# Moving the GpSimd additions of the first three pairs of an MLP product to VectorE

## Chip, cores and metric

The kernel runs on one core of a Trainium2 chip. The metric is device time in microseconds for one launch: the median of the runs shown. Beside it stands one profiled execution, from which the rows of the profile come. The engines are TensorE (PE in the profile; its weight loads PEld), VectorE (DVE), ScalarE (ACT), GpSimd (POOL) and SyncE (SP), whose queue issues the loads and stores.

## What is computed

Two layers of a hybrid block on 1024 latent tokens and 256 context tokens of width 1024. Each layer has a modulated norm, an input projection, a mixture of attention, Fourier and gated position mixing, an output projection with a gated residual, and then the part that matters here:

```python
def squared_relu_mlp(h, w1, w2):
    return jnp.square(jax.nn.relu(h @ w1)) @ w2

x = x + gt1 * mix_x
x = x + gt2 * squared_relu_mlp(modulate(rms_norm(x, g2), sh2, sc2), w1, w2)
```

`w1` is 1024 x 4096. The context goes through the same weights in layer 0 only; layer 1 (`last` in the code) leaves it out. Everything is float32.

## The kernel before

**Precision.** A float32 product is made of three TensorE products: each operand is split into a rounded part `h` (a ScalarE copy that rounds) and a rest `lo` (a VectorE subtraction), and `h*h`, `h*lo`, `lo*h` are summed in PSUM. So every operand tile costs one ScalarE and one VectorE instruction of 128x512 before TensorE can use it.

**Quads and blocks.** The latent tokens form two quads of 512 tokens (`QUADS`). The first MLP product is done by Strassen's scheme on 2 x 2 blocks: the features in two halves of four 128-chunks, the tokens in two quads, and the 4096 columns of `w1` in pairs (block `p` and block `p + NP`, `NP` = 16), so that 7 block products replace 8. Its operand sums are formed once for the tokens (lists `ysum[1..7]`) and once per pair for the weights (`split_block`). The stages that the change touches, in the order of the code:

- `mix_out` (L1329) adds the output projection to the residual and calls `square_sum` (L502, L503): ScalarE squares a chunk, GpSimd adds it to the quad's sum of squares. The sum over all 8 chunks (`KC`) goes through ones-matmuls (L522) to the row statistics.
- `norm_first` and `norm_second` modulate the chunks of quad 0 and quad 1 (`modulated`, L1470 and L1471), form the sums of chunks (`y_sum`, L1482) and split each into `h` (L1476) and `lo` (L1477) in `y_split`. `c in YSUM`, which is chunk 1 or 3, goes to GpSimd, the others to VectorE; all four sums of `norm_first` carry the number 1.
- `split_block` forms a weight sum (L1582; on GpSimd for the products named in `FSUM` from pair 2 on) and splits it (L1584, L1586).
- `first_product` issues the 12 matmuls of one block product (L1672 to L1674; context L1658 to L1660).
- `after_product` copies products 2, 5, 1 from PSUM (L1688), forms their sums (L1690 on VectorE, L1692 on GpSimd, L1696, L1700, L1703, L1707 from PSUM on VectorE) and applies the squared ReLU (L1643, L1644).
- `combine` forms five sums (L1635) of a pair's four result blocks, the operand sums of the second product, and stores them; sums number 1 and 3 (`POOLT`) are on GpSimd.

The order of products is a list written out by hand, `seq`: products of the first three pairs (0, 1, 2) are interleaved, since the token sums are still being formed; `norm_second` is a generator (`side2`) stepped beside the first two pairs by `ahead_of`, and weight splits run three items ahead. From pair 3 on all operands of the tokens exist. The order in each engine's queue is not the order of the source: a scheduler orders the instructions before they are run, by readiness and by their place in the source. Each queue is then run in order.

Of the kernel before, what the change touches and what calls it, by code (L numbers as in the profile page):

```python
# [15 lines left out]
ALU = mybir.AluOpType  # L16
# [4 lines left out]
KC = D // P  # L21
# [6 lines left out]
NP = NFF // 2  # L28
POOLT = (1, 3)
FSUM = ((2, 1, 6), (2, 6))  # L30
YSUM = (1, 3)
HD = 64
NH = 8
EPS = 1e-6
# [95 lines left out]
def hybrid_block_kernel(ctx: ExitStack, tc: tile.TileContext, a: dict, out: bass.AP):  # L130
# [10 lines left out]
    def alloc(tag, shape, dt):  # L141
        cnt[0] += 1
        tag_of[f"{tag}_{cnt[0]}"] = tag
        return sb.tile([P] + list(shape), dt, tag=tag, bufs=BUFS[tag], name=f"{tag}_{cnt[0]}")
# [7 lines left out]
    def T(*shape, dt=F32R):  # L152
        return alloc("T", shape, dt)

    def M(*shape, dt=F32):
        return alloc("M", shape, dt)
# [9 lines left out]
    def PB(*shape, dt=F32):  # L166
        cnt[0] += 1
        tag_of[f"pB_{cnt[0]}"] = "B"
        return ps.tile([P] + list(shape), dt, tag="B", bufs=8, name=f"pB_{cnt[0]}")
# [4 lines left out]
    V, A, E, G = nc.vector, nc.scalar, nc.tensor, nc.gpsimd  # L174
# [20 lines left out]
    def mm3(o, lh, ll, rh, rl, first, last):  # L195
        E.matmul(o, lh, rh, start=first, stop=False)  # L196
        E.matmul(o, lh, rl, start=False, stop=False)  # L197
        E.matmul(o, ll, rh, start=False, stop=last)  # L198
# [293 lines left out]
            y[1].append(lo)  # L492
            yield

    def square_sum(acc, x, k):

        w = x.w
        if k == 0:
            A.activation(acc[:, :w], x.chunk(k), AF.Square)
        else:  # L500
            sq = M(512)
            A.activation(sq[:, :w], x.chunk(k), AF.Square)  # L502
            G.tensor_tensor(acc[:, :w], acc[:, :w], sq[:, :w], ALU.add)  # L503

    def norm(x, acc, mod, j, y, pool=False):

# [116 lines left out]
    def layer(l, ys, norms, bank):  # L623
# [84 lines left out]
        for pi in range(5):  # L708
            ts = (2 * pi, 2 * pi + 1)
            w = 512 if ts[0] in tiles else 256  # L710
# [607 lines left out]
        def mix_out(x, wts, qi, d):  # L1318

            hs, ls = wts  # L1320
            o = PB(512)
            for i, k in enumerate(MIX_ORDER):
                f = slice((k % 4) * P, (k % 4 + 1) * P)
                mm3(o[:, :x.w], hs[k // 4][:, f], ls[k // 4][:, f], *mix[qi, k], i == 0, i == KC - 1)
                if i % 3 == 2:
                    yield
            yield
            j = 0 if qi < 2 else 1
            V.scalar_tensor_tensor(x.chunk(d), o[:, :x.w], mods[l, 2][:, j, d:d + 1], x.chunk(d), ALU.mult, ALU.add)  # L1329
            square_sum(ssum[qi], x, d)  # L1330

        class Two(Rows):

# [4 lines left out]
        ssum = {}  # L1338

        def early_out(qs):  # L1340

            x = {}
            for qi in qs:
                yield from split_mix(qi, MIX_ORDER)
                ssum[qi] = S(512)
                x[qi] = Two(qi)
                xmid[qi] = DR(f"xm_{l}_{qi}", P, KC * x[qi].w)
            ahead = [split_rows(a["w_out"][l], 0, WTAG[0], G if WG[l] else V)]
            for d in range(KC):
                wts = ahead.pop(0)  # L1350
                if d + 1 < KC:
                    ahead.append(split_rows(a["w_out"][l], d + 1, WTAG[(d + 1) % 2], G if WG[l] else V))
                for qi in qs:
                    if d % 2 == 0:
                        w = x[qi].w
                        t = R(2, w) if qi == 0 else S(2, w)
                        load(flat(t), xdram[l, qi][:, d * w:(d + 2) * w])
                        x[qi].t.append(t)
                yield
                for qi in qs:  # L1360
                    yield from mix_out(x[qi], wts, qi, d)
                    if d % 2:
                        w = x[qi].w
                        store(xmid[qi][:, (d - 1) * w:(d + 1) * w], flat(x[qi].t[d // 2]))
            yield from split_mix(1, [k for k in MIX_ORDER if k != 3])
            wout.append(split_rows(a["w_out"][l], 0, WTAG[0]))
            yield
            wout.append(split_rows(a["w_out"][l], 1, WTAG[1]))
            yield
# [110 lines left out]
        def y_sum(c, x, y, op):  # L1480
            t = M(512)
            (G if c in YSUM else V).tensor_tensor(t, x, y, op)  # L1482
            return t
# [110 lines left out]
        for d in range(KC):  # L1594
            if d + 2 < KC:
                wout.append(split_rows(a["w_out"][l], d + 2, WTAG[d % 2]))
            if d == KC - 3:
                w1_load(0, 0)
                w1_load(1, 0)
                w1_load(0, 1)  # L1600
                w1_load(2, 1, "T")
                split_block(5, 0, "T")
            if d == KC - 2:
                w1_load(1, 1)
                split_block(5, 1, "T")
                split_next()
                split_next()
            if d == KC - 1:
                split_next()
            for i, _ in enumerate(mix_out(xm[1], wout[d], 1, d)):  # L1610
                step(side)
                if last and i == 1 and d:
                    to_tokens(1, d - 1)
            if d % 2 and not last:
                store(xmid[1][:, (d - 1) * 512:(d + 1) * 512], flat(xm[1].t[d // 2]))
# [7 lines left out]
        def put(i, p, t):  # L1623
            store(tdram[i][:, p * 512:(p + 1) * 512], t)

        def combine(p):

            b11, b12, b21, b22 = (hq.pop((p, b)) for b in (11, 12, 21, 22))
            put(2, p, b11)
            put(5, p, b22)  # L1630
            for n, (i, x, y, op) in enumerate(((4, b21, b11, ALU.subtract), (3, b12, b22, ALU.subtract),
                                               (1, b11, b22, ALU.add), (6, b11, b12, ALU.add),
                                               (7, b21, b22, ALU.add))):
                t = alloc("W2", [512], F32)
                (G if n in POOLT else V).tensor_tensor(t, x, y, op)  # L1635
                put(i, p, t)

        fbank, fsum = {}, {}
        BANK = {2: "a", 4: "a", 5: "g", 3: "g", 1: "b", 7: "b", 6: "d"}

        def relu2(p, b, src, t=None):
            t = t or T(512, dt=F32)
            A.activation(t, src, AF.Relu)  # L1643
            A.activation(t, t, AF.Square)  # L1644
            hq[p, b] = t
# [38 lines left out]
        def after_product(i, p):  # L1684
            o = fbank[p, BANK[i]]
            if i in (2, 5, 1):
                m = fsum[p, i] = alloc("T" if (i, p) == (2, 2) else "W2", [512], F32)
                A.copy(m, o)  # L1688
            if i == 5:
                V.tensor_tensor(fsum[p, 2], fsum[p, 2], fsum[p, 5], ALU.add)  # L1690
            if i == 1:
                G.tensor_tensor(fsum[p, 1], fsum[p, 1], fsum[p, 2], ALU.subtract)  # L1692
            if i in (4, 5):
                fsum[p, "n"] = fsum.get((p, "n"), 0) + 1
                if fsum[p, "n"] == 2:
                    V.tensor_tensor(fsum[p, 5], fbank[p, "a"], fsum[p, 2], ALU.subtract)  # L1696
                    relu2(p, 21, fbank[p, "a"])
            if i == 7:
                t = T(512, dt=F32)
                V.tensor_add(t, o, fsum[p, 5])  # L1700
                relu2(p, 11, t, t)
            if i == 3:
                V.tensor_add(fsum[p, 1], o, fsum[p, 1])  # L1703
                relu2(p, 12, o)
            if i == 6:
                t = T(512, dt=F32)
                V.tensor_add(t, o, fsum[p, 1])  # L1707
                relu2(p, 22, t, t)
                combine(p)
# [166 lines left out]
        def finish_quad(qi):  # L1876

            x = xm[qi]
            nsum[qi] = S(512)
            for k in range(KC):  # L1880
                square_sum(nsum[qi], x, k)
                yield
            keep(l + 1, qi, x)
            nnorm[qi] = norm(x, nsum[qi], lambda: (mods[l + 1, 1], mods[l + 1, 0]), 0 if qi < 2 else 1, ny[qi],
                             qi == 0)
            if qi == 0:
                yield from nnorm[0]
# [45 lines left out]
        if not last:  # L1933
            finish_bg()

            x = xm[2]
# [94 lines left out]
```

## Time and profile before

| quantity | value |
|---|---|
| runs | 2709.23, 2714.17, 2719.12 us; median 2714.17 |
| profiled execution | 2711.95 us, span 2710.2 us |
| mean granted TensorE clock | 0.989 |
| GpSimd instructions | 773 |
| VectorE instructions | 3709 |
| L1482 on GpSimd | 24 of 40, median 1.30 us, longest 5.29 us |
| L1482 on VectorE | 16 of 40, median 0.68 us, longest 1.78 us |

Times in the profile are microseconds unless marked ns; `pB` is a PSUM tile, all other names are tiles in SBUF or tensors in DRAM. "idle before" is the engine's idle time ahead of a group and, behind the arrow, the instruction that ended it. A chain is the sequence of work that ended last, each piece released by the one before it.

### The profile page before, as it was taken

The numbers are of one execution on the slowest core, as the hardware profiler recorded it, in microseconds if no ns is written. First come the engines' busy times: TensorE is split into PE (matmuls) and PEld (weight loads), VectorE is DVE, ScalarE is ACT, GpSimd is POOL, SyncE is SP. The second block draws the span as 40 slices with busy tenths as digits, with TensorE's granted clock in tenths as the row PEclk, the third lists the DMA queues.
The fourth block names the chain that finished last, engine by engine and source line by source line (L and its number), as shares of the span: only waits on it lengthen the run. The fifth ranks groups of instructions, "written<-read, shape, count | busy, mean of one in ns | idle before, by whom it ended". The sixth has DMA issues, their size and how long they took to land.

```text
span 2710.2 us, 39517 instructions
## 1 busy us (share of the span) xinstructions
PE 2597.2 (96%) x13236; PEld 2140.0 (79%) x13236; DVE 2177.7 (80%) x3709; ACT 1526.1 (56%) x3248; POOL 1013.1 (37%) x773
## 2 busy tenths in 40 slices
PE   7998899999989999999999999899999899999999
PEld 4777687787768888888879987787886688888877
DVE  7897979768998998689887674888676877766598
ACT  6636878656454445444455434888775555554443
POOL 4321745511253333145452101543323444324486
PEclk9999999999999999999999999999999999999999
DMA  8535231326144554786558323231352444485454
GB/s 283 173 112 150 75 96 38 117 71 195 58 140 156 161 184 161 265 303 202 187 158 299 109 79 119 67 96 46 101 161 78 160 142 153 152 303 192 142 174 138
DMA packets 316492, 406.13 MB, mean 150 GB/s; under 512 B 24040, under 2 KB 204672, under 8 KB 316288
## 3 DMA queue, kind: packets, MB, share of 16 engines
q1 hardware_dynamic: 311136, 394.43, 44.8%
q0 software_dynamic: 5152, 9.18, 1.2%
q8 instruction: 104, 1.70, 0.3%
q14 instruction: 100, 0.82, 0.1%
HBM read 299.97 MB, written 103.55 MB: 149 GB/s over the span
## 4 chain that ended last, share of the span: by engine, by line
PE 74%; DVE 14%; ACT 4%; issue 3%; DMA 3%; POOL 2%; SPq 0%; DVEq 0%; ACTq 0%; POOLq 0%
PE pB L196 11%; PE pB L197 11%; PE pB L198 11%; PE pB L1674 7%; PE pB L1672 7%; PE pB L1673 7%; PE pB L1145 4%; PE pB L1158 2%; PE pB L1159 2%; PE pB L1066 2%; PE pB L1067 2%; PE pB L1980 1%; PE pB L1979 1%; PE pB L1978 1%; DVE pB L353 1%
## 5 line engine op out<-in xcount | busy, mean ns | idle before, releaser
L1747 ACT CAST T<-R 128x512 fp32r<-128x512 f32 x224 | 139.0, 622 | 293.4 <-PE pB L197 278.8
L1748 DVE TENSOR_TENSOR T<-R,T 128x512 fp32r<-128x512 f32 x224 | 196.4, 878 | 94.6 <-ACT T L1747 94.4
L1148 DVE TENSOR_TENSOR T<-pB,T 128x512 fp32r<-128x512 f32 x328 | 223.1, 684 | 51.2 <-ACT T L1147 47.4
L1147 ACT CAST T<-pB 128x512 fp32r<-128x512 f32 x328 | 195.0, 600 | 69.3 <-PE pB L1145 34.4
L1674 PE MATMUL pB<-S,W 128*128 128x512 f32 x496 | 197.3, 398 | 3.4 <-DVE W L1586 3.4
L1112 DVE TENSOR_REDUCE mb<-pB 128x1 f32<-128x512 f32 x256 | 172.4, 682 | 33.1 <-PE pB L1067 32.0
L1672 PE MATMUL pB<-S,W 128*128 128x512 f32 x496 | 198.0, 399 | 0.0
L1673 PE MATMUL pB<-S,W 128*128 128x512 f32 x496 | 197.2, 398 | 0.6 <-DVE S L1477 0.6
L1754 POOL TENSOR_TENSOR M<-W,S 128x512 f32<-128x512 f32 x96 | 147.9, 1546 | 129.6 <-DVE W L1758 74.4
L1635 POOL TENSOR_TENSOR W<-T,T 128x512 f32<-128x512 f32 x64 | 110.4, 1745 | 204.2 <-issue 86.3
L1758 DVE TENSOR_TENSOR W<-M,W 128x512 fp32r<-128x512 f32 x160 | 182.7, 1142 | 0.0
L1128 ACT ACTIVATE L<-pB,nm 128x512 f32<-128x512 f32 x256 | 178.8, 704 | 0.1
L197 PE MATMUL pB<-W,T 128*128 128x512 f32 x448 | 175.6, 392 | 2.8 <-DVE W L1758 2.8
L198 PE MATMUL pB<-T,W 128*128 128x512 f32 x448 | 175.8, 392 | 1.2 <-DVE W L1758 1.0
L196 PE MATMUL pB<-T,W 128*128 128x512 f32 x448 | 176.0, 393 | 0.0
L197 PE MATMUL pB<-T,W 128*128 128x512 f32 x448 | 174.6, 390 | 1.4 <-DVE T L1748 1.4
L198 PE MATMUL pB<-W,T 128*128 128x512 f32 x448 | 174.6, 390 | 1.2 <-DVE T L1748 1.2
L196 PE MATMUL pB<-W,T 128*128 128x512 f32 x448 | 174.4, 389 | 0.0
L1145 PE MATMUL pB<-ident,L 128*128 128x128 f32 x1056 | 162.2, 276 | 10.5 <-DVE T L1148 4.6
L1145 PEld LDWEIGHTS pB<-ident,L 128*128 128x128 f32 x1056 | 127.5, 141 | 50.0 <-DVE T L1148 8.8
L1672 PE MATMUL pB<-L,W 128*128 128x512 f32 x384 | 154.1, 402 | 12.5 <-ACT W L1584 9.4
L353 DVE SCALAR_TENSOR_TENSOR pB<-A,sil,pB 128x256 f32<-128x256 f32 x266 | 156.4, 603 | 8.2 <-DMA A<-in_w_ada 4.7
(356 smaller groups left out, 8170.6 us busy)
## 6 DMA issues: line engine op xcount, KB each, us to landing
R<-t SPq DMA_DIRECT2D x112, 512.0 KB, 4.0
W<-in_w_mlp SPq DMA_DIRECT2D x160, 256.0 KB, 3.1
t<-W SPq DMA_DIRECT2D x160, 256.0 KB, 2.3
S<-in_w_mlp SPq DMA_DIRECT2D x128, 256.0 KB, 5.1
A<-in_w_ada SPq DMA_DIRECT2D x112, 256.0 KB, 3.1
R<-in_w_mlp SPq DMA_DIRECT2D x48, 512.0 KB, 4.5
R<-in_w_out SPq DMA_DIRECT2D x32, 512.0 KB, 4.2
t<-T SPq DMA_DIRECT2D x64, 256.0 KB, 2.0
```

The costliest lines, as they stand in the source:

```text
L196: E.matmul(o, lh, rh, start=first, stop=False)
L197: E.matmul(o, lh, rl, start=False, stop=False)
L198: E.matmul(o, ll, rh, start=False, stop=last)
L353: V.scalar_tensor_tensor(ac[j], w[:, kk, :], s, ac[j], ALU.mult, ALU.add)
L1145: E.transpose(tp[:, b * P:(b + 1) * P], src, ident)
L1147: A.copy(ph, tp)
L1148: V.tensor_sub(pl, tp, ph)
L1672: E.matmul(o, h[:, cs], yh, start=(new and c == 0), stop=False, skip_group_check=True)
L1673: E.matmul(o, h[:, cs], yl, start=False, stop=False, skip_group_check=True)
L1674: E.matmul(o, lo[:, cs], yh, start=False, stop=(c == 3), skip_group_check=True)
L1748: V.tensor_sub(tl, src, th)
L1758: V.tensor_sub(sl, s, sh)
```

## The change

Five places, none of which changes what is computed. `YSUM` becomes empty, so all sums of `y_sum` are formed on VectorE. `square_sum` gets an argument that puts the addition of the last chunk of quad 1 on VectorE. In `combine` the two GpSimd sums, and in `after_product` the GpSimd subtraction for product 1, go to VectorE in pairs 0, 1 and 2; from pair 3 on they stay on GpSimd. GpSimd keeps the weight sums of pair 2 and the other square sums.

```diff
-YSUM = (1, 3)
+YSUM = ()
...
-    def square_sum(acc, x, k):
+    def square_sum(acc, x, k, fast=False):
...
-            G.tensor_tensor(acc[:, :w], acc[:, :w], sq[:, :w], ALU.add)
+            (V if fast else G).tensor_tensor(acc[:, :w], acc[:, :w], sq[:, :w], ALU.add)
...
-            square_sum(ssum[qi], x, d)
+            square_sum(ssum[qi], x, d, qi == 1 and d == KC - 1)
...
                 t = alloc("W2", [512], F32)
-                (G if n in POOLT else V).tensor_tensor(t, x, y, op)
+                (G if n in POOLT and p > 2 else V).tensor_tensor(t, x, y, op)
                 put(i, p, t)
...
             if i == 1:
-                G.tensor_tensor(fsum[p, 1], fsum[p, 1], fsum[p, 2], ALU.subtract)
+                (G if p > 2 else V).tensor_tensor(fsum[p, 1], fsum[p, 1], fsum[p, 2], ALU.subtract)
```

## The prediction

> **What bounds the kernel now.** I read the page's shares first, then the chain of work that ended last, then busy time by stage, then the groups of VectorE (DVE) and GpSimd (POOL) instructions inside the stages that the diff touches.
>
> ```profile
> span 2710.2 us, 39517 instructions
> ...
> PE 2597.2 (96%) x13236; PEld 2140.0 (79%) x13236; DVE 2177.7 (80%) x3709; ACT 1526.1 (56%) x3248; POOL 1013.1 (37%) x773
> ...
> PE 74%; DVE 14%; ACT 4%; issue 3%; DMA 3%; POOL 2%; SPq 0%; DVEq 0%; ACTq 0%; POOLq 0%
> ```
>
> TensorE (PE) is busy for 96% of the span and carries 74% of the chain, so a microsecond counts only where TensorE waits. The diff touches two short stretches, one per layer: the start of the first MLP product. They lie at about 664 to 830 us (layer 0) and 2010 to 2165 us (layer 1). The answer of busy time by stage (engine busy and count, then the granted TensorE clock, DMA share and GB/s) shows them:
>
> ```profile
> core 0: us, PE busy (x) PEld busy (x) DVE busy (x) ACT busy (x) POOL busy (x), PEclk, DMA share, GB/s
> 664.00:712.00 48.00, 43.33 (x179) 34.63 (x178) 45.65 (x83) 20.61 (x38) 16.75 (x12) 0.94 0.36 113
> 712.00:783.00 71.00, 60.87 (x312) 49.07 (x311) 64.17 (x83) 41.47 (x75) 28.90 (x16) 0.99 0.24 81
> 783.00:850.00 67.00, 67.00 (x353) 57.25 (x352) 54.54 (x70) 33.01 (x57) 27.95 (x19) 1.00 0.46 148
> 2061.00:2088.00 27.00, 23.79 (x104) 18.43 (x103) 21.57 (x35) 14.79 (x29) 10.06 (x5) 1.00 0.19 59
> 2088.00:2112.00 24.00, 17.04 (x50) 11.62 (x50) 20.15 (x30) 14.19 (x25) 8.40 (x5) 0.79 0.10 34
> 2112.00:2136.00 24.00, 18.56 (x62) 13.36 (x62) 19.68 (x22) 9.77 (x17) 11.09 (x7) 0.86 0.75 232
> ```
>
> In 712 to 783 TensorE idles 71 - 60.9 = 10.1 us, in 2061 to 2136 it idles 75 - 59.4 = 15.6 us: 25.7 us in all, the ceiling for what shorter waits can give. VectorE is near full there (64.2 of 71; 61.4 of 75). From 783 on TensorE is busy for all of 67 us, so what is won before 783 is carried on and not waited away at once. The chain between 716 and 783 (start us, us, what) runs nearly wholly over VectorE, with GpSimd in it:
>
> ```profile
> 725.96 5.30 POOL M L1482
> ...
> 738.43 0.60 DVE M L1482
> ...
> 753.83 1.69 DVE M L1482
> ...
> 761.88 5.50 DMA R<-in_w_mlp
> ...
> 782.66 0.39 PE pB L1660
> ```
>
> The same line stands in layer 1's chain:
>
> ```profile
> 2075.96 4.10 POOL M L1482
> ...
> 2101.13 4.12 POOL M L1482 x2
> ```
>
> L1482 is y_sum, the operand sums. On VectorE one takes 0.60 us of the chain when undisturbed and 1.69 when not; the GpSimd ones hold the chain for 5.30, 4.10 and (two) 4.12 us. The next two answers, VectorE groups of 712 to 783 and of 2061 to 2132 (count, busy us, mean ns, then idle before), tell why:
>
> ```profile
> L1477 DVE TENSOR_TENSOR L<-M,L 128x512 fp32r<-128x512 f32 x12 | 11.5, 989 | 0.0
> L1586 DVE TENSOR_TENSOR W<-M,W 128x512 fp32r<-128x512 f32 x9 | 8.2, 921 | 0.0
> L1482 DVE TENSOR_TENSOR M<-L,L 128x512 f32<-128x512 f32 x8 | 8.1, 1016 | 0.0
> L1635 DVE TENSOR_TENSOR W<-T,T 128x512 f32<-128x512 f32 x6 | 7.2, 1231 | 0.0
> ...
> L1582 DVE TENSOR_TENSOR M<-R,R 128x512 f32<-128x512 f32 x4 | 3.2, 805 | 0.0
> L1477 DVE TENSOR_TENSOR S<-M,S 128x512 fp32r<-128x512 f32 x4 | 2.7, 680 | 1.8 <-ACT S L1476 1.8
> ...
> L1707 DVE TENSOR_TENSOR T<-pB,W 128x512 f32<-128x512 f32 x2 | 1.4, 680 | 0.0
> ```
>
> ```profile
> L1477 DVE TENSOR_TENSOR L<-M,L 128x512 fp32r<-128x512 f32 x12 | 11.0, 939 | 2.0 <-ACT L L1476 1.8
> L1586 DVE TENSOR_TENSOR W<-M,W 128x512 fp32r<-128x512 f32 x10 | 8.9, 903 | 0.8 <-ACT W L1584 0.8
> L1635 DVE TENSOR_TENSOR W<-T,T 128x512 f32<-128x512 f32 x6 | 7.3, 1222 | 0.2 <-ACT T L1644 0.2
> L1482 DVE TENSOR_TENSOR M<-L,L 128x512 f32<-128x512 f32 x8 | 6.8, 854 | 0.2 <-ACT L L1471 0.2
> ...
> L1477 DVE TENSOR_TENSOR S<-M,S 128x512 fp32r<-128x512 f32 x4 | 3.1, 787 | 1.8 <-ACT S L1476 1.8
> ```
>
> All these are additions or subtractions of 128x512. Where one operand comes from PSUM (pB, L1707) the mean is 680 ns; where both lie in SBUF the same operation averages up to 1231. Those are the ones that a GpSimd tensor_tensor disturbs, and GpSimd in turn suffers, as its group of 712 to 783 shows (mean 2016 ns, against 1.29 us for one that runs undisturbed, quoted below):
>
> ```profile
> L1482 POOL TENSOR_TENSOR M<-L,L 128x512 f32<-128x512 f32 x8 | 16.1, 2016 | 31.4 <-ACT L L1471 21.4 <-DVE S L1477 6.3 <-DVE W L1586 1.9
> L1635 POOL TENSOR_TENSOR W<-T,T 128x512 f32<-128x512 f32 x4 | 6.4, 1622 | 3.5 <-ACT T L1644 3.5
> L1582 POOL TENSOR_TENSOR M<-R,R 128x512 f32<-128x512 f32 x2 | 3.4, 1711 | 9.1 <-DMA R<-in_w_mlp 9.1
> L1692 POOL TENSOR_TENSOR W<-W,W 128x512 f32<-128x512 f32 x2 | 3.1, 1537 | 1.6 <-ACT W L1688 1.6
> ```
>
> **The change, part by part.** Per layer 22 instructions go from GpSimd to VectorE: 12 y_sum (4 in norm_first, 8 in norm_second), 1 square sum, 3 of L1692, 6 of the combinations L1635. Of these, 8 + 2 + 4 = 14 lie in the bound stretch of each layer; L1582 of pair 2 stays (2 of the 16 GpSimd instructions in the window).
>
> Bound stretch, layer 0. Added to VectorE: 14 x 0.60 = 8.4 us. Given back: the excess of the disturbed groups over 680 ns, 12 x 0.309 + 9 x 0.241 + 8 x 0.336 + 6 x 0.551 + 4 x 0.125 = 12.4 us, of which 14 of 16 instructions' share goes: 10.9. Also the 1.8 us in which VectorE stood idle for a ScalarE cast (L1476) that waited for GpSimd's 5.30 us sum. Net 8.4 - 10.9 - 1.8 = -4.3 us. The 5.50 us DMA in the chain is a load into an R buffer that an earlier VectorE sum frees, so I let it move with the chain and count nothing.
>
> Layer 1. Added 8.4; excess 12 x 0.259 + 10 x 0.223 + 6 x 0.542 + 8 x 0.174 + 4 x 0.107 = 10.4, by the same 14/16 share 9.1; two idle times of VectorE behind late sums, 1.8 + 1.8. Net -4.3 us.
>
> The Trainium skill ("SBUF — State Buffer", section "SBUF: two separate sides") says that VectorE with two SBUF inputs and GpSimd take turns at one port pair and that the loser is blocked for the whole instruction. The rows agree in kind: 10.9/14 is 0.78 us per GpSimd instruction. By that rule a VectorE instruction could lose up to the whole 1.29 us each time, 14 x 1.29 = 18.1 us a layer, and the net would be -11.5 us in layer 0; I go by the rows.
>
> Clock. In layer 1 the waits below are long, and the granted clock behind them is 0.79 and 0.86, which is 0.21 x 24 + 0.14 x 24 = 8.4 us of clock lost:
>
> ```profile
> 2088.47 0.80 PE L1672 MATMUL pB<-L,W 128*128 128x512 f32 x1 [3.04 <-ACT W L1584]
> ...
> 2096.82 0.49 PE L1672 MATMUL pB<-L,W 128*128 128x512 f32 x1 [2.03 <-ACT W L1584]
> ...
> 2111.47 0.50 PE L1672 MATMUL pB<-L,W 128*128 128x512 f32 x1 [3.07 <-ACT W L1584]
> ```
>
> Waits that shrink give some clock back. Bounds 0 and 8.4; I take 2 us, near the lower end, since a part of the faster clock would only lengthen the next wait on VectorE.
>
> norm_first and the square sum (664 to 712, layer 0). VectorE is busy 45.7 of 48 us, so four sums add 4 x 0.60 = 2.4. Against that stand two GpSimd sums that the chain passes through here and the last square sum; GpSimd's rows in order of time show the second sum and the square sum,
>
> ```profile
> 677.84 1.29 POOL L1482 TENSOR_TENSOR M<-L,L 128x512 f32<-128x512 f32 x1 [0.62 <-ACT L L1471]
> ...
> 704.98 1.31 POOL L503 TENSOR_TENSOR T<-T,M 128x512 f32<-128x512 f32 x1 [5.00 <-ACT M L502]
> ```
>
> each 0.7 us shorter on VectorE if VectorE is free when its input comes. The square sum now makes VectorE wait for ScalarE's square; behind it are queued the modulation products of the next layer and the weight splits, and TensorE's row statistics wait for it. I take 0, with -2.1 (three on the chain, 0.7 each) and +2.4 as ends. In layer 1 TensorE does not wait there: its first wait after 2010 falls behind 2061, and VectorE has room. Nothing.
>
> L1692 on VectorE must wait for ScalarE's copy of the product; behind it are queued the y subtractions (L1477) and weight splits (L1586), for which TensorE waits. GpSimd stood 1.6 us before it. VectorE at that place has its backlog to work off before it gets there, so I take 0; ends 0 and +1.6 a layer. Pair 2's three moved instructions per layer lie where TensorE does not wait (783 to 850; VectorE 54.5 of 67 busy): +1.8 us of VectorE, covered. If the cover went, 1.8 a layer would show. The stores of the combined tiles stay on SP's queue in their places; GpSimd's own queue has less before L1582, which can only start earlier.
>
> Sum: -4.3 - 4.3 - 2 + 0 = -10.6 us. The profiled execution took 2711.95 us (span 2710.2 and 1.75 around it); that becomes 2701.4. It stands 2.2 us below the median of the runs, 2714.17, so the forecast against the median is 2703.6 us, 0.39% less. About 0.3%, 8.1 us, is what a measurement of this kernel can tell from no change.
>
> **The rivals.**
> 1. The clock comes back wholly. If all waits of layer 1 fall well under 3 us and no slow matmul follows, 8.4 us return in place of 2: 2697.2 us. For it: the waits of 3.04 and 3.07. Against it: a wait of 2.03 lies in the slow stretch too. The Trainium skill ("TensorE: Matmul & The Clock Gate", "Why this matters for your kernels") has the rule that gaps over about 3 us bring half clock, which would favour this rival; the trace leaves it open.
> 2. The round trip shows. A sum on VectorE is followed by a ScalarE cast and a VectorE subtraction of the same tile; with both ends on one in-order queue VectorE can stand idle for the cast, about 0.7 us (a cast of some 0.6 and two hand-offs). If 8 of the 16 moved sums show this, 5.6 us go, and the time is 2709.2: within 0.3%. Against it: the eight sums of each layer already on VectorE cause almost no idle time before L1477 today (the rows' idle is that behind GpSimd). For it: today the other half runs beside them, which leaves VectorE work to fill in.
> 3. One layer's gain is given back at a later wait (a weight load that does not move with the chain, such as the 5.50 us DMA): 2714.17 - 6.3 = 2707.9 with layer 1's gain alone.
> 4. VectorE becomes the bound, slower than before. The place is L1477 and L1586 in the two stretches: if their excess is not GpSimd's doing (TensorE and ScalarE read the same tiles), 16.8 us are added and only the 5.4 us of idle return: 2725.6 us. It decides when a moved instruction gives back less than (16.8 - 5.4)/28 = 0.41 us; the rows say (10.9 + 9.1)/28 = 0.71. Against it stands the PSUM row of 680 ns in the same stretch.
>
> **How the numbers follow.** Forecast 0.46, rival 1 0.12, rival 2 0.22, rival 3 0.08, rival 4 0.12. The forecast's own range is 2699 to 2710: from the front's -2.1 with two or three more from the clock, to the front's +2.4 with L1692's two 1.6. About four fifths of its chance lies below 2706, so faster is 0.46 x 0.8 + 0.12 = 0.49; within 0.3% is the rest of it with rivals 2 and 3, 0.39; slower 0.12. The range runs from 2691 (rival 1 with the port rule's extra or the front's gain) to 2716 (the forecast with all its upper ends and a round trip); it leaves out rival 4 and tails.
>
> **What would show it.** VectorE has 44 instructions more (3753), GpSimd 44 less (729). No GpSimd instruction of L1482; in the two stretches L1477, L1482 and L1635 on VectorE average 680 to 750 ns. TensorE's idle time in the stretch before the stall-free part falls from 10.1 to about 6 us in layer 0 and from 15.6 to about 9 in layer 1, with a granted clock above 0.9. The chain there has no POOL of 4 to 5 us. It is wrong if the means stay near 950 (rival 4), if VectorE's idle before L1477 grows by several us (rival 2), if TensorE starts to wait behind 783, or if the stall before the statistics of the second quad (L522) grows by more than 2 us.

## The result and the profile after

The kernel after takes 2694.14 us (median; 2687.71 to 2695.27) against 2712.36 us before in the same comparison: a ratio of 0.9923, 95% interval 0.9910 to 0.9936. That is 0.77% faster, 21 us by the ratio. The forecast was 2703.6 us with a range of 2691 to 2716: sign and range held, the gain was put too low by some 8 to 10 us, and the forecast's own narrower range, 2699 to 2710, was missed. The profiled execution after took 2694.72 us.

The page of the kernel after, shares by engine:

```profile
span 2692.5 us, 39484 instructions
...
PE 2596.2 (96%) x13236; PEld 2142.9 (80%) x13236; DVE 2172.8 (81%) x3753; ACT 1528.8 (57%) x3248; POOL 940.4 (35%) x729
```

VectorE runs 44 instructions more and is busy 5 us less (2172.8 against 2177.7): over the whole span the moved work cost it no busy time. Busy time by stage, after, with the same stretches and columns as in the prediction:

```profile
664.00:712.00 48.00, 47.24 (x215) 38.22 (x215) 47.39 (x92) 22.68 (x42) 10.34 (x7) 1.00 0.36 116
712.00:783.00 71.00, 65.57 (x335) 53.53 (x334) 69.02 (x106) 45.48 (x80) 7.95 (x5) 0.98 0.33 104
783.00:850.00 67.00, 67.00 (x354) 57.17 (x353) 53.52 (x75) 30.84 (x55) 23.51 (x15) 1.00 0.42 142
...
2052.00:2127.00 75.00, 66.08 (x254) 49.58 (x254) 65.58 (x108) 43.79 (x77) 6.33 (x4) 0.91 0.37 115
```

Layer 1's stretch now begins 8.4 us earlier, so its 75 us are 2052 to 2127. TensorE's idle time fell from 10.1 to 5.4 us in 712 to 783 and from 15.6 to 8.9 us in layer 1, about as forecast (6 and 9). What was not forecast is the first row: in 664 to 712 TensorE was busy 43.33 us at a clock of 0.94, and is now busy 47.24 us at 1.00. VectorE's groups of 704 to 776 after:

```profile
L1482 DVE TENSOR_TENSOR M<-L,L 128x512 f32<-128x512 f32 x16 | 10.8, 693 | 0.0
L1477 DVE TENSOR_TENSOR L<-M,L 128x512 fp32r<-128x512 f32 x12 | 8.0, 697 | 0.0
L1586 DVE TENSOR_TENSOR W<-M,W 128x512 fp32r<-128x512 f32 x10 | 8.0, 797 | 0.8 <-ACT W L1584 0.7
...
L1635 DVE TENSOR_TENSOR W<-T,T 128x512 f32<-128x512 f32 x10 | 6.4, 686 | 0.0
...
L1582 DVE TENSOR_TENSOR M<-R,R 128x512 f32<-128x512 f32 x4 | 3.9, 967 | 0.0
```

L1477, L1482 and L1635, which averaged 989, 1016 and 1231 ns, are at 686 to 697, and the idle time behind ScalarE's casts before L1477 is gone. The two groups that are still long stand beside the two weight sums of pair 2 that stay on GpSimd.

To see where the time went I cut the spans at landmarks of TensorE: the transposes (L475) for the context's norm, the row statistics (L522) and transposes of the second quad, the last matmul of the first MLP product (L1674), and the last two in layer 1. Two of these, before and after, as TensorE's rows in order of time show them:

```profile
667.95 0.41 PE L475 MATMUL pB<-ident,M 128*128 128x128 f32 x2 [0.76 <-DVE M L471]
706.34 1.86 PE L522 MATMUL pB<-ones,T 128*128 128x1 f32 x8 [3.91 <-POOL T L503]
```

```profile
669.63 0.41 PE L475 MATMUL pB<-ident,M 128*128 128x128 f32 x2 [0.76 <-DVE M L471]
703.96 0.95 PE L522 MATMUL pB<-ones,T 128*128 128x1 f32 x8
```

38.39 us between them became 34.33, and the wait of 3.91 us is gone. All kernels, one profiled execution each, in us from start to start:

| kernel | L475 to L522 | L522 to L475 | to the last matmul, layer 0 | L475 to the last matmul, layer 1 | ratio to before |
|---|---|---|---|---|---|
| before | 38.39 | 9.52 | 411.25 | 325.80 | 1 |
| after | 34.33 | 6.48 | 407.49 | 317.32 | 0.9923 |
| e1 products held | 36.50 | 8.14 | 412.98 | 325.03 | 0.9989 |
| e2 first norm | 36.74 | 9.70 | 411.34 | 325.43 | 0.9979 |
| e3 second norm | 38.39 | 9.10 | 408.74 | 320.31 | 0.9953 |
| e4 pairs | 38.39 | 9.19 | 412.17 | 320.17 | 0.9976 |
| e5 first norm, square | 34.33 | 6.48 | 412.16 | 326.93 | 0.9970 |
| e6 square | 38.10 | 9.71 | 411.21 | 324.82 | 0.9996 |
| e7 idle sums on GpSimd | 34.32 | 6.49 | 414.03 | 325.32 | 0.9985 |
| e8 extra sums on VectorE | 38.40 | 8.99 | 419.10 | 326.95 | 1.0036 |
| e9 weight sums of pair 2 | 34.32 | 6.48 | 407.13 | 315.67 | 0.9920 |
| e10 all squares of quad 1 | 34.28 | 6.48 | 408.79 | 316.99 | 0.9918 |
| e11 held, square | 35.96 | 8.14 | 411.32 | 325.91 | 0.9985 |
| e12 both of e9, e10 | 34.28 | 6.48 | 407.80 | 316.11 | 0.9923 |

Kernels that leave the third part alone agree on it within 1.8 us (411.2 to 413.0), on the fourth within 2.1 (324.8 to 326.9). The parts come from one execution each and the ratios from all runs; the profiled execution of the kernel before (2711.95 us) lies below the medians that the ratios are taken against (2712.36 to 2714.63), so the parts can add up to less than a ratio says. The change won 4.06 + 3.04 us in the front of layer 0, 3.76 in its bound stretch and 8.48 in layer 1: 19.3 of a span that is 17.7 shorter, the rest being 1.7 us lost ahead of the first landmark, where nothing is changed, and 0.1 between the others.

### The profile page after: what moved, and what is told of

Same layout as the page of the kernel before. It is cut to its first block, busy times and chain, and to the rows that moved or that the text cites. A ratio compares the mean times of both kernels' runs of the same rounds, so it can differ in the third digit from the quotient of the medians.

```text
span 2692.5 us, 39484 instructions
## 1 busy us (share of the span) xinstructions
PE 2596.2 (96%) x13236; PEld 2142.9 (80%) x13236; DVE 2172.8 (81%) x3753; ACT 1528.8 (57%) x3248; POOL 940.4 (35%) x729
## 5 line engine op out<-in xcount | busy, mean ns | idle before, releaser
L1674 PE MATMUL pB<-S,W 128*128 128x512 f32 x496 | 197.4, 398 | 2.1 <-DVE W L1586 2.1
L353 DVE SCALAR_TENSOR_TENSOR pB<-A,sil,pB 128x256 f32<-128x256 f32 x266 | 154.9, 599 | 8.6 <-DMA A<-in_w_ada 5.0
L1672 PE MATMUL pB<-L,W 128*128 128x512 f32 x384 | 153.8, 401 | 7.4 <-ACT W L1584 7.4
L1674 PE MATMUL pB<-L,W 128*128 128x512 f32 x384 | 153.4, 400 | 3.9 <-DVE W L1586 3.9
```

The source lines that it names most:

```text
L1672: E.matmul(o, h[:, cs], yh, start=(new and c == 0), stop=False, skip_group_check=True)
L1674: E.matmul(o, lo[:, cs], yh, start=False, stop=(c == 3), skip_group_check=True)
```

## The experiments

Two theories of the gain in the bound stretches are set against each other. The port theory says that a GpSimd addition lengthens the VectorE additions beside which it runs. The wait theory says that only the late results of GpSimd mattered, for which ScalarE's casts waited.

**e7, unread sums on GpSimd.** The kernel after, with sums on GpSimd that nothing reads.

```diff
             (G if c in YSUM else V).tensor_tensor(t, x, y, op)
+            if c in (1, 3):
+                for h in range(2):
+                    hs = slice(h * 256, (h + 1) * 256)
+                    G.tensor_tensor(vg, x[:, hs], y[:, hs], op)
...
-                    y_split(4, y_sum(1, x, xm[0].chunk(k - 4), ALU.subtract), S)
+                    y_split(4, y_sum(0, x, xm[0].chunk(k - 4), ALU.subtract), S)
```

`YSUM` is empty, so the sums that are used are all on VectorE; the sums of `norm_first` now carry the number 0, so only those of `norm_second` are repeated.

> The kernel after the change, with GpSimd also forming the eight second-quad sums per layer that it formed before, in two halves, into a tile that nothing reads; VectorE's order around the modulation products is that after the change. Nobody waits for these. Port theory: each costs VectorE some 0.7 us in the bound stretches, 5 to 6 us a layer: the kernel loses 6 to 12 of the 21 us and VectorE's L1477 and L1482 climb to 800 to 950 ns. Wait theory (the gain is that ScalarE no longer waits for late GpSimd sums): nothing lost, within 3 us of the kernel after.

Measured 2710.68 us, ratio 0.9985 (0.9976 to 0.9994): 17 of the 21 us are lost again. The order of instructions in VectorE's and ScalarE's queues is the same as after the change. But it is not so that nobody waits for the sums. Nobody reads them, yet they read tiles into which ScalarE's casts (L1476) write next, and the list of waits (us in total, times, longest) shows three casts that waited for them:

```profile
ACT L L1476 <- POOL vg L1486: 8.4, 3, 3.9
```

So e7 puts back both things, the contention and some waiting, and the two have to be told apart by the rows. VectorE's and GpSimd's rows in order of time (in e7 the line numbers behind the new sum, L1486, are 4 higher: L1590 is L1586):

```profile
716.05 0.69 DVE L1482 TENSOR_TENSOR M<-L,L 128x512 f32<-128x512 f32 x1
716.66 1.23 DVE L1477 TENSOR_TENSOR S<-L,S 128x512 fp32r<-128x512 f32 x1
717.81 0.68 DVE L1590 TENSOR_TENSOR W<-W,W 128x512 fp32r<-128x512 f32 x1
718.41 1.23 DVE L1477 TENSOR_TENSOR S<-L,S 128x512 fp32r<-128x512 f32 x1
719.56 1.23 DVE L1482 TENSOR_TENSOR M<-L,L 128x512 f32<-128x512 f32 x1
```

```profile
715.38 1.96 POOL L1486 TENSOR_TENSOR vg<-L,L 128x256 f32<-128x256 f32 x2 [16.72 <-ACT L L1471]
718.23 6.63 POOL L1486 TENSOR_TENSOR vg<-L,L 128x256 f32<-128x256 f32 x6 [0.89 <-POOL vg L1486]
```

An undisturbed 0.68 becomes 1.23 beside a half-wide sum, and six half-wide sums of GpSimd take 6.63 us. In layer 0 the groups of e7 (704 to 783) are:

```profile
L1482 DVE TENSOR_TENSOR M<-L,L 128x512 f32<-128x512 f32 x16 | 11.8, 750 | 0.0
L1477 DVE TENSOR_TENSOR L<-M,L 128x512 fp32r<-128x512 f32 x12 | 8.4, 727 | 2.1 <-ACT L L1476 2.1
L1590 DVE TENSOR_TENSOR W<-R,W 128x512 fp32r<-128x512 f32 x11 | 8.0, 731 | 0.0
...
L1477 DVE TENSOR_TENSOR S<-L,S 128x512 fp32r<-128x512 f32 x4 | 4.4, 1092 | 0.0
L1477 DVE TENSOR_TENSOR S<-M,S 128x512 fp32r<-128x512 f32 x4 | 3.3, 814 | 0.0
```

Since the order is the same, VectorE's rows can be set against those of the kernel after one by one. In layer 0 the 121 that begin between 704 and 776 us after the change take 3.5 us longer in e7, and VectorE stands idle 2.1 us longer, behind one of the three casts; the stretch is 6.4 us longer (rows overlap a little, so the two do not add up exactly), and the third landmark part 6.5 (414.03 against 407.49). In layer 1 the 108 between 2052 and 2127 take 5.5 us longer and idle 1.9 us more, and the part is 8.0 us longer. So some 9 of the 14.5 us are longer rows, inside the 6 to 12 us that the port theory expected, and some 4 us are a wait that it had left out. The wait theory can account for that wait and not for the longer rows. The means rose less than expected (727 to 814 for most groups, not 800 to 950): few rows are hit (10 of the 121 by more than 0.15 us), but on the path. TensorE's granted clock in 712 to 783 also fell, from 0.98 to 0.93; what that alone cost, these runs do not tell.

That it is GpSimd which lengthens the rows, and not TensorE or ScalarE (rival 4), the trace of the kernel before shows by itself. It has 1250 VectorE tensor_tensor rows of 128x512 with no operand in PSUM. 731 of them have no GpSimd tensor_tensor running beside them, and none of these takes more than 696 ns. The other 519 have one, and 319 of these take more than 800 ns, up to 1811. Of the rows with an operand from PSUM, 225 have one beside them, and the longest takes 693 ns.

**e8, the price of added sums.** The kernel before, with the eight sums per layer that GpSimd forms formed once more on VectorE, in halves, into the same unread tile.

> The kernel before, with VectorE also forming (in two halves, into a tile that nothing reads) the eight sums per layer that GpSimd forms in norm_second: the price of the moved sums without anything given back. If VectorE is the bound there: 16 x 0.7 = 11 us, less what falls into its 1.8 and 3.6 us of idle time and its waits for TensorE in layer 1: 4 to 11 us more than before. If VectorE has room: within 2 us.

Measured 2723.09 us, ratio 1.0036 (1.0023 to 1.0049): 10 us slower, inside the first theory's 4 to 11. The landmarks put 7.9 us in layer 0 and 1.2 in layer 1. The sixteen half sums are busy for 11.5 us in layer 0 (718 ns each, where the median of all is 414, since GpSimd's sums run beside them) and for 8.2 us in layer 1. So in the kernel before added work on VectorE shows for the greater part in layer 0's stretch and hardly at all in layer 1's, where the sum counted the same 8.4 us. It is not VectorE's time alone: the granted clock in 712 to 783 is 0.88, against 0.99 before.

**e3 and e4, the two parts of the stretch.**

```diff
-YSUM = (1, 3)
+YSUM = ()
...
-            (G if c in YSUM else V).tensor_tensor(t, x, y, op)
+            (G if c in YSUM or c == 9 else V).tensor_tensor(t, x, y, op)
...
-                    y_split(4, y_sum(1, x, xm[0].chunk(k - 4), ALU.subtract), S)
+                    y_split(4, y_sum(9, x, xm[0].chunk(k - 4), ALU.subtract), S)
```

In e3, above, number 9 marks the sums of `norm_first`, which stay on GpSimd. e4 is:

```diff
-                (G if n in POOLT else V).tensor_tensor(t, x, y, op)
+                (G if n in POOLT and p > 2 else V).tensor_tensor(t, x, y, op)
...
-                G.tensor_tensor(fsum[p, 1], fsum[p, 1], fsum[p, 2], ALU.subtract)
+                (G if p > 2 else V).tensor_tensor(fsum[p, 1], fsum[p, 1], fsum[p, 2], ALU.subtract)
```

> Only the eight sums of norm_second per layer go to VectorE. Port theory: 8 of 14 shares of the excess, 6.2 and 5.2 us, and the idle times of 1.8 and 3.6 us come back for 4.8 us added in each layer: -3.2 in layer 0 and -4.0 in layer 1, 5 to 10 us less in all; VectorE's L1477 falls below 800 ns. Wait theory (only ScalarE's waits for late GpSimd sums mattered, the long VectorE rows did not): 9.6 us added for 5.4 won: 0 to 4 us more than before.

Measured 2703.47 us, ratio 0.9953 (0.9940 to 0.9966), 13 us less: more than the 5 to 10 expected. By landmarks 2.5 us in layer 0 (expected 3.2) and 5.5 in layer 1 (expected 4.0). In layer 1 the twelve L1477 rows average 768 ns, below 800 as the port theory expected. The sign speaks against the wait theory as it was priced; by e8 that price was too high in layer 1, so the plainer evidence is layer 0, where it expected a loss.

> Only the sums of the first three pairs (two of combine, and the subtraction for product 1) go to VectorE. Port theory: 6 of 14 shares of the excess, 4.7 and 3.9 us, for 3.6 us added in each layer: 0 to 3 us less than before. If the first MLP product's start were bound by VectorE's plain count of instructions, 3 to 7 us more.

Measured 2708.22 us, ratio 0.9976 (0.9966 to 0.9986), 6.5 us less where 0 to 3 were expected. Layer 0 shows nothing (412.17 against 411.25), layer 1 shows 5.6 us. TensorE's waits at the end of layer 1's stretch in e4:

```profile
2121.25 0.50 PE L1672 MATMUL pB<-S,W 128*128 128x512 f32 x1 [0.25 <-ACT W L1584]
2122.30 0.50 PE L1672 MATMUL pB<-S,W 128*128 128x512 f32 x1 [0.32 <-ACT W L1584]
2128.18 0.50 PE L1672 MATMUL pB<-L,W 128*128 128x512 f32 x1 [0.23 <-ACT W L1584]
2130.87 0.50 PE L1674 MATMUL pB<-L,W 128*128 128x512 f32 x1 [1.96 <-DVE W L1586]
```

They come to 2.8 us; before, the waits there were 0.89, 0.56, 1.02 and 2.61, together 5.1. The two parts win 11.1 us in layer 1 by themselves and 8.5 together, so they overlap. In layer 0 they win 1.6 us by themselves and 3.8 together, a difference no greater than the two parts' scatter of 1.8 us can make.

**e1, e2, e5, e6, e11, the front of layer 0.** In the queue order that the scheduler makes, 9 modulation products (L353) stood between the last two residuals (L1329) of the second quad before the change, and 4 after. Counted from 640 us on, 26 stood ahead of the last residual before the change and 19 after. Nothing in the diff touches them; the four sums of norm_first take the places on VectorE that products had filled (e2, which moves only these, has the same 4 and 19). e1 changes this order alone, by a dependency of the 15th product on the last residual:

```diff
+    last_res, nprod, HOLD = [], [0], 15
...
+                        if last_res:
+                            nprod[0] += 1
+                            if nprod[0] == HOLD:
+                                tc.add_manual_dep(tc.nc.cur_bb.bb.instructions[-1], last_res[0].name,
...
+            if l == 0 and qi == 1 and d == KC - 1:
+                last_res.append(tc.nc.cur_bb.bb.instructions[-1])
```

> The kernel before, with nothing moved off GpSimd: only VectorE's order is changed. From the 15th accumulating modulation product (L353 of before) on, these products may not stand before the last residual of quad 1 (L1329 of before) in layer 0; before the change 9 of them stand between the last two residuals, here 3, after the change 4. Order theory: the front's gain in layer 0 (the wait before L522 and the slow clock behind it, 7.1 us between the two profiles) came from these products going behind, not from GpSimd: this kernel takes 4 to 7 us less than before, all in layer 0 ahead of the stretch at 712 us, with no wait of TensorE above 1 us before L522. Port theory for the front: the gain came from GpSimd sums no longer disturbing VectorE there: this kernel gains 0 to 1 us.

In the trace 4 products stand between the last two residuals, not 3, and 21 ahead of the last. Measured 2711.3 us, ratio 0.9989 (0.9981 to 0.9998), 3 us less, between the two theories. The landmarks show 1.9 us before L522 and 1.4 behind it; a wait is left:

```profile
708.91 1.05 PE L530 MATMUL pB<-ones,T 128*128 128x1 f32 x8 [2.02 <-POOL T L511]
```

(In e1 the line numbers are 8 higher: L530 is L522, L511 is L503.) So the order explains part of the front, 3.3 of the 7.1 us, and not all.

> Only the four sums of norm_first per layer go to VectorE; the sums of norm_second, the pairs' sums and the square sum stay on GpSimd. Order theory: the four sums take VectorE's free places in the planned order and so push the modulation products behind the last residual (4 between the last two residuals, as after the change); 4 to 7 us less, in layer 0 only, and the same as the kernel that only holds the products back, within 2 us. Port theory: at most 1.4 us given back for 2.4 us added: 0 to 1 us more than before.

e2 puts the first norm's sums on VectorE and nothing else: 2709.46 us, ratio 0.9979 (0.9970 to 0.9988), 6 us less, as the order theory expected for the whole. But by landmarks only 1.65 us lie before L522 and none behind it, against 1.9 and 1.4 in e1. Another 2.4 us lie ahead of the first landmark, where nothing is changed; 1.6 of them come from a spell of slow clock (654 to 658 us) that comes or stays away from one execution to the next. GpSimd, VectorE, TensorE and the clock in e2's front:

```profile
698.62 3.62 POOL L503 TENSOR_TENSOR T<-T,M 128x512 f32<-128x512 f32 x1 [4.21 <-ACT M L502]
```

```profile
697.67 2.85 DVE L353 SCALAR_TENSOR_TENSOR pB<-A,sil,pB 128x256 f32<-128x256 f32 x7
```

```profile
702.30 1.37 PE L522 MATMUL pB<-ones,T 128*128 128x1 f32 x8 [2.26 <-POOL T L503]
```

```profile
700.00:712.00 12.00, 9.74 (x33) 0.72 0.22 68
```

The residual is now early, but the square sum on GpSimd takes 3.62 us beside seven products in a row, TensorE waits 2.26 us, and the granted clock over the 12 us around and behind that wait is 0.72.

> Only the square sum of the last chunk of quad 1 on VectorE. The order of the modulation products ahead of the last residual stays as before (9). Joint theory: the wait of 3.91 us before L522 falls by 0.7 us only, since the residual itself is late; slow clock stays: 0 to 2 us less. If the square sum alone were what made the front, 5 to 7 us less.

e6: 2712.33 us, ratio 0.9996 (0.9987 to 1.0006). Nothing measurable, 0.3 us in the landmark. Alone, the square sum does not matter, since the residual is late.

> The two edits of the front together: norm_first's sums and the last square sum of quad 1 on VectorE; norm_second and the pairs stay on GpSimd. With norm_first's sums alone TensorE still waited 2.26 us before L522, because the square sum on GpSimd took 3.62 us beside a run of modulation products on VectorE. Joint theory: with the square sum on VectorE that wait goes and the slow clock behind it with it, as after the change: 5 to 8 us less than before, no wait before L522, granted clock 1.00 there. Additive theory: the square sum gives only its 0.7 us: 5 us less at most, with a wait of 1 to 2 us left before L522.

e5: 2705.35 us, ratio 0.9970 (0.9959 to 0.9980), 8 us less. The landmarks are those after the change to 0.01 us (34.33 and 6.48): the two edits win 7.1 us together over both front parts, where apart they win 1.5 and 0.1. The joint theory holds; the rows of e2 show why.

> The held products of the first experiment with the last square sum of quad 1 on VectorE; norm_first's sums stay on GpSimd. If norm_first's sums worked in the front only through the order of the modulation products, this kernel has the front of the kernel with both front edits (34.3 us from the context's transposes to L522 and 6.5 from there to the next, against 38.4 and 9.5 before): no wait of TensorE before L522, 5 to 8 us less than before. If the GpSimd sums of norm_first also held VectorE up there, a wait of about 1 to 2 us is left, with or without slow clock: 2 to 5 us less.

e11: 2708.82 us, ratio 0.9985 (0.9976 to 0.9994). The parts are 35.96 and 8.14 us, and a wait of 1.47 us before L522 is left: the second case. Holding the products and moving the square sum gives 3.8 of the 7.1 us. The other 3.3 come with norm_first's sums leaving GpSimd; which of the two does it, the long VectorE rows beside those sums or the two products that e11 still has earlier (21 ahead of the last residual, not 19), these runs do not separate.

**e9, e10, e12, going further.** From the kernel after: the weight sums of pair 2 to VectorE (`p > 2` in `split_block`), all square sums of the second quad to VectorE (`qi == 1`), and both.

> The kernel after the change, with the weight sums of pair 2 on VectorE too, so that GpSimd has nothing left in the two bound stretches. Port theory: after the change VectorE's L1586 and L1582 beside the weight sums that stay on GpSimd still average 823 and 967 ns, some 2 us of excess in layer 0 and 1 in layer 1, for 2 and 1 sums at 0.6 us: 0 to 3 us less than the kernel after (ratio to before 0.991 to 0.9925). If it is slower than the kernel after by more than 2 us, the added sums lie on the bound.

> The kernel after the change, with all square sums of quad 1 on VectorE, not only the last. In layer 0 the front has no wait of TensorE left to win; six more sums push modulation products (14 where 19 stood) behind the last residual, into the stretch where VectorE is the bound: 5 x 0.4 = 2 us more there, against 2 us of GpSimd disturbance gone in the front. Expected within 3 us of the kernel after (ratio 0.9912 to 0.9935); if the products in the bound stretch are what costs, 2 to 3 us slower.

> The kernel after the change with both additions of the last two experiments: the weight sums of pair 2 and all square sums of quad 1 on VectorE. Each alone stood at the kernel after within the interval (ratios 0.992 and 0.9918 against 0.9923). Expected the same again or up to 3 us less: ratio 0.991 to 0.993.

Ratios 0.9920 (0.9906 to 0.9934), 0.9918 (0.9904 to 0.9931) and 0.9923 (0.9909 to 0.9936): all three stand where the kernel after stands (0.9923). e9's landmarks show 0.4 and 1.6 us less, within the scatter of the parts; e10 shows 1.3 more in layer 0's stretch, where the products pushed back now lie, and that too is within it. No version beats the kernel after.

## Why the prediction was right, and where it was short

- **Bound stretch, layer 0: -4.3, measured -3.76.** Right in mechanism and close in size. The rows of the kernel before and e7 show that the excess is GpSimd's doing, and by the groups after it fell from 12.4 to about 3 us, with the idle 1.8 us gone as well. That the 8.4 us added count nearly in full is less firmly shown: of e8's 11.5 us of added work 7.9 show. With a scatter of 1.8 us between kernels, agreement within 0.6 us is partly luck.
- **Bound stretch, layer 1: -4.3, and -2 for the clock; measured -8.48.** For the clock, 0.89 over the 75 us is 8.4 us lost before and 0.91 is 6.8 after, so 1.6 us came back, near the 2 assumed. That agreement is luck: e1 and e6, which leave this stretch alone, have as much clock as the kernel after (0.93 over 2050 to 2150, against 0.91 before). The rest gave more than 4.3, and the term most likely mis-sized is "added 8.4": e8 finds only 1.2 us for 8.2 us of added work there. VectorE was busy 61.4 of 75 us, so added work could fall into its idle time, and the 8.4 of layer 0 should not have been used again unbounded. This is argued and not shown: e8 prices work in the kernel before, where GpSimd's late sums hold the chain (4.10 and 4.12 us), and how much came from their going these runs do not separate.
- **The front of layer 0: 0 with ends -2.1 and +2.4; measured -7.1, outside the ends.** This is the step that failed. It priced the moved instructions (0.7 us each) and held the order of VectorE's queue fixed. The order changed: seven products fewer ahead of the last residual, five of them from between the last two residuals (e1, with five fewer and nothing moved: 1.9 us before L522 and 1.4 behind it). It took the square sum for 1.31 us, where GpSimd needs 3.62 beside a run of products (e2), so that only both edits together remove the wait (e5). And it gave the slow clock behind a wait of 3.91 us no term of its own: 3.04 us of the 7.1 lie behind L522. The measured time still fell inside the stated range because its lower end, 2691, made room for the whole clock with an extra; that this covered gains in other places is luck.
- **Rival 1, the whole clock back:** did not come. One wait is as long as before, and the clock behind it is low:

```profile
2086.16 0.79 PE L1672 MATMUL pB<-L,W 128*128 128x512 f32 x1 [3.24 <-ACT W L1584]
```

  The Trainium skill ("TensorE: Matmul & The Clock Gate", "Why this matters for your kernels") lets gaps of over about 3 us bring half clock. This wait agrees. In e2 a wait of 2.26 us was enough, with a clock of 0.72 around it, and in e11 one of 1.47 us, with 0.79 over the 8.1 us behind it. The kernel before has a wait of 1.74 us at 746 us and a clock of 1.00 from 730 to 780. So below 3 us the length of a wait alone does not decide here.
- **Rival 2, the round trip:** no idle time before L1477 after the change. **Rival 3, given back later:** from 783 to 850 TensorE is busy 67.00 of 67, and layer 0's gain stands whole to the start of layer 1 within 1 us. **Rival 4, VectorE as the bound:** added work does show in layer 0, as e8 finds, but its condition fails, since the excess is GpSimd's doing.
- **Port or wait:** the prediction read the long rows as GpSimd's doing from means alone. The rows of the kernel before, with and without a GpSimd addition beside them, make it a finding. e7 gives its price: with both queues in the same order, sums that nobody reads cost 17 us, 14.5 of them in the two stretches, of which some 9 are longer rows and some 4 casts that waited.

## What to carry to other kernels

Where a second engine's additions make VectorE's rows twice as long, moving them to VectorE can be free: here 44 moved instructions left its busy time 5 us lower, and putting unread ones back on GpSimd cost 17 us. An unread instruction is not a free probe: it still holds the tiles that it reads, so ask who waits for it. Price an added instruction stretch by stretch: here the same sixteen half sums cost 7.9 us in one and 1.2 in the other. When a scheduler makes the queue order, compare the orders as well as the durations: here some 7 us came where four sums displaced other work ahead of a wait, 3.3 of them by the order alone, and two edits that were worth 1.5 and 0.1 us apart were worth 7.1 together.

## What the runs showed of the hardware

GpSimd is held up for longer than one VectorE instruction. A sum that takes 1.29 us when undisturbed took 5.29 from 725.96 on (before): beside it seven VectorE rows of 0.68 us ran one behind the other until 730.1, and it ended 1.15 us after them. The square sum took 3.62 (e2). The VectorE products of e2 (L353) read one tile from SBUF, a scalar column and one tile from PSUM, and they are disturbed too, while another instruction with the same kinds of operands (L1470) is not. The rows of L353 and of L1470 in the kernel before (min, median, max ns):

```profile
L353 DVE SCALAR_TENSOR_TENSOR pB<-A,sil,pB x266: 424/479/1530, 162.8 to 1308.7; 128x256 f32<-128x256 f32 x133
...
L1470 DVE SCALAR_TENSOR_TENSOR M<-L,mod,pB x32: 728/742/748, 654.5 to 2099.1; 128x512 f32<-128x512 f32 x32
```

L353 goes to three times its median beside GpSimd (1.53 us at 698.7, with a square sum running from 698.4 to 700.0): 207 of its 266 rows have no GpSimd addition beside them and take at most 490 ns, and of the 59 others 35 take more than 800. L1470 never leaves 742 by more than 14 ns, and 11 of its 32 rows have a GpSimd addition beside them. The Trainium skill ("SBUF — State Buffer", "SBUF: two separate sides") names two SBUF inputs or a two-port mode as the condition; the additions agree with that, L353 does not, and no run here tells what sets it apart: it writes to PSUM, L1470 to SBUF.
